# A list of 381 displacements in the issue order of a two-layer encoder

## The chip, the cores and the metric

The kernel runs on one core of a Trainium2 chip. The metric is the time of one execution on the device in microseconds, the median of several runs. One execution is profiled; its rows are what this document argues from. The engines are TensorE (PE; its weight loads are listed as PEld), VectorE (DVE), ScalarE (ACT), GpSimd (POOL) and SyncE (SP, which issues DMAs).

## The reference

Two transformer layers over 1024 tokens of width 1024, in float32. Layer 0 has two groups of heads: A, eight heads of grouped-query attention with normalised and rotated q and k, and B, eight heads of latent attention whose keys and values come from a 128-wide latent. Layer 1 has 16 heads of attention in a window of 128 tokens to each side, with a distance penalty and a sink. Both are gated by SiLU, and each layer has an adaptive normalisation in front.

```python
for layer in range(DEPTH):
    mod = c_act @ ada_w[layer] + ada_b[layer]
    shift, scale, gate = jnp.split(mod, 3, axis=-1)
    h = rms_norm(x, norm_w[layer]) * (1.0 + scale[:, None, :]) + shift[:, None, :]
    y = even_mixer(h, ...) if layer % 2 == 0 else odd_mixer(h, ...)
    x = x + gate[:, None, :] * y
return rms_norm(x, final_norm)
...
# one head of either group of layer 0
sc = jnp.einsum('bqkgd,bskd->bkgqs', qi, k).astype(jnp.float32) * scale
p = jax.nn.softmax(sc, axis=-1).astype(v.dtype)
o = jnp.einsum('bkgqs,bskd->bqkgd', p, v)
```

## The kernel before

**Numbers in two parts.** A float32 operand is split into a rounded part ("hi", fp32r) and the rest ("lo"). The name of a tile ends in h or l for them, or the two lie in one tile (hl, hla, hlb: 512 columns each). A product is then two or three fp32r matmuls.

**Stages.** Layer 0's input projections run first (to about 140 us), then the heads of group A (to about 425 us), those of group B (to about 650 us), the output projection of layer 0 in a scheme with seven instead of eight quarter products (`wino_out`), the projections and windowed heads of layer 1, and its output projection. `run_groups` treats half a head (512 queries) as a group. For each of its four blocks of 128 queries `softmax_unit` makes the scores S (matmuls into two PSUM banks), their negated row maximum nm (a reduction on DVE), the exponential P with its row sum sm (ACT), the reciprocal rs (DVE) and the scaling of P (POOL). For the group before, `pv_step` runs eight times: four transposes of P into a PSUM tile (named T), a cast to hi (ACT, left half of hla in group A and of hlb in group B), the rest lo (DVE, right half), and two matmuls with the values VA or VB into an accumulator pv. `pv_final` adds the accumulator's two halves (ot on ACT, og on DVE) and gates (POOL). Gate projections (gT), the modulation vectors (ada, adag: a reduction over a loaded tile on DVE), and group B's q and k halves (q, k, VB, qrt, cqTh) are filled in between.

**What sets the order.** No instruction is issued where the code writes it. A `Recorder` (`add`, `cost`, `run`) notes 9556 operations in the order of the code, each with its number i, its engine, an estimated duration and the operations that it depends on. `run` is a list scheduler: it plays the five engines with those durations, gives every engine the ready operation of lowest priority number, gives out PSUM banks and SBUF slots as they come free, and keeps an instruction of DVE with two SBUF inputs from starting while POOL is busy, and the reverse (`held`). What it returns is a start time for each operation. `emit` sorts by these starts, passes the sequence through `moved` and `banks_in`, and issues the operations in that sequence. Each engine runs its own operations strictly in that order, and an operation waits for its inputs and for the bank or slot that it writes.

**moved** (from line 488) takes the list `MOVES` of triples (kind, i, j). Kind 0 brings operation i forward to just before j, with all operations between them that i depends on; kind 1 puts i back to just after j, with all operations between them that depend on i:

```python
for kind, i, j in moves:
    lo, hi = (pos[j], pos[i]) if kind == 0 else (pos[i], pos[j])
    group, todo = {i}, [i]
    while todo:
        x = todo.pop()
        near = [d for d in self.ops[x].deps if d >= 0] if kind == 0 else [u for u, full in self.ops[x].users if full]
        for d in near:
            if d not in group and lo <= pos[d] <= hi:
                group.add(d)
                todo.append(d)
    here, rest = [x for x in part if x in group], [x for x in part if x not in group]
    seq[lo:hi + 1] = here + rest if kind == 0 else rest + here
```

**banks_in** walks the final sequence and keeps the bank that `run` gave to a PSUM tile where it is still free there, and else takes another free one (the one that has been free longest, for a pair of banks). So a displacement can also change the bank of a tile, and with it the instruction that the tile's first writer waits for.

In this kernel `MOVES` is empty: the sequence is the list scheduler's own, and every tile has the bank that `run` gave it. Since all operations are issued from one helper, all rows of the profile bear one line (L551); they are told apart by the names of their tiles.

Of the kernel before, what the change touches and what calls it, by code (L numbers as in the profile page):

```python
# [70 lines left out]
ADA_AT = (8, 5, ("c2", 6), 2, 4, 10, ("op", 1, 7), ("w", 2, 2))  # L71


MOVES = ()

SLOPES = [float(np.float32(2.0) ** np.float32(-8.0 * k / 16)) for k in range(1, 17)]

# [37 lines left out]
class Recorder:  # L115
# [427 lines left out]
    def emit(self):  # L543
        total = self.run()
        real = lambda v: v.real() if isinstance(v, VP) else v
        seq = self.moved([o.i for o in sorted(self.ops, key=lambda o: (o.start, o.i))], MOVES)
        self.banks_in(seq)
# [1506 lines left out]
```

## Time and profile before

| What | Value |
|---|---|
| Median of 3 runs | 1178.45 us (1177.72 to 1179.77) |
| The profiled execution's own time | 1180.8 us |
| Its span, first to last instruction | 1178.1 us |
| Mean granted clock of TensorE | 0.992 |
| Busy: PE, DVE, ACT, POOL | 1140.4, 948.4, 699.9, 599.9 us |
| DMA | 133.42 MB, mean 113 GB/s |

A row of the timeline or of a group reads: start (or count), duration, engine, line, operation, written tile<-read tiles, shapes, and in square brackets the idle time of the engine before it with what ended it. A row of windows reads: stretch, its length, then for PE, PEld, DVE, ACT and POOL the busy time with the number of instructions, then the granted clock of PE, the busy share of the DMA engines and the GB/s they moved. The waits that ended PE's idle time, summed by releaser over the heads of layer 0 (110 to 660 us), are:

```profile
PE psum L551 <- DVE hla L551: 6.5, 8, 1.7
PE psum L551 <- ACT Pa L551: 4.5, 5, 1.9
PE psum L551 <- DVE hlb L551: 1.5, 5, 0.5
PE psum L551 <- DVE q L551: 1.2, 3, 0.8
PE psum L551 <- ACT Pb L551: 1.0, 3, 0.4
```

The columns are the total in us, the number of waits and the longest one.

### The profile page before, as it was taken

Reading aid. Unit: us, or ns where it says so; the run is one execution under the profiler, and the core shown is the slowest. Engines: PE = TensorE matmul, PEld = TensorE weight load, DVE = VectorE, ACT = ScalarE, POOL = GpSimd, SP = SyncE. Lnnn points to the kernel's source line nnn. Section 1 sums busy time; section 2 is a strip of 40 time slices with the busy share of each in tenths; the row PEclk is TensorE's granted clock in tenths of the full one; section 3 lists DMA queues with packets and bytes.
Section 4 is the critical chain, followed back from the end, with each engine's and each line's share of the span. In section 5 each row is a group of like instructions: output and inputs, shape, how many; then the busy total and the mean of one; then the engine's idle time right before and its main releaser. Section 6 shows DMA issues by size and latency. Waiting matters only on the chain.

```text
span 1178.1 us, 17460 instructions
## 1 busy us (share of the span) xinstructions
PE 1140.4 (97%) x6070; PEld 957.6 (81%) x6070; DVE 948.4 (81%) x1678; ACT 699.9 (59%) x1406; POOL 599.9 (51%) x579
## 2 busy tenths in 40 slices
PE   7999999999999999999999999999999999999996
PEld 7898877878877878788877887988888888888885
DVE  8974889888887988888889988959776597765885
ACT  5553356565555777787778832327765365565723
POOL 1334496957854645554445444704465266445414
PEclk9999999999999999999999999999999999999998
DMA  9601433232221148786125333400002212036413
GB/s 368 253 1 66 163 117 125 90 111 89 84 63 54 52 116 222 186 217 175 37 88 225 117 143 125 161 19 8 31 18 91 72 37 90 19 144 237 139 35 143
DMA packets 41671, 133.42 MB, mean 113 GB/s; under 512 B 4592, under 2 KB 9200, under 8 KB 41584
## 3 DMA queue, kind: packets, MB, share of 16 engines
q1 hardware_dynamic: 38192, 122.88, 29.4%
q0 software_dynamic: 2304, 8.39, 4.2%
q8 instruction: 47, 0.77, 0.3%
q10 hardware_dynamic: 1088, 1.05, 0.3%
q14 instruction: 40, 0.33, 0.1%
HBM read 101.24 MB, written 31.06 MB: 112 GB/s over the span
## 4 chain that ended last, share of the span: by engine, by line
PE 77%; DVE 11%; ACT 5%; DMA 3%; issue 2%; POOL 1%; SPq 0%; POOLq 0%; ACTq 0%; DVEq 0%
PE psum L551 77%; DVE nm L551 2%; DMA ada<-in_ada_t 2%; DMA w2s<-in_w_c 1%; DMA w31s<-in_w_c 1%; ACT k L551 1%; DVE hla L551 1%; ACT Pa L551 1%; ACT q L551 1%; DVE adag L551 1%; DVE xr L551 1%; ACT Pb L551 1%; DVE hl L551 1%; DVE p L551 0%; DVE hlb L551 0%
## 5 line engine op out<-in xcount | busy, mean ns | idle before, releaser
L551 DVE TENSOR_REDUCE nm<-psum 128x1 f32<-128x1024 f32 x128 | 154.6, 1217 | 16.4 <-PE psum L551 14.7
L551 POOL TENSOR_SCALAR p<-p,dn 128x384 f32<-128x384 f32 (+1 forms) x128 | 71.8, 580 | 154.9 <-ACT p L551 74.6
L551 PE MATMUL psum<-hla,VA 128*128 128x512 f32 x256 | 94.1, 427 | 9.0 <-DVE hla L551 6.5
L551 POOL TENSOR_SCALAR Pa<-Pa,rs 128x1024 f32<-128x1024 f32 x64 | 78.9, 1238 | 43.4 <-DVE rs L551 41.3
L551 POOL TENSOR_SCALAR Pb<-Pb,rs 128x1024 f32<-128x1024 f32 x64 | 72.1, 1128 | 41.6 <-DVE rs L551 39.6
L551 ACT CAST hla<-psum 128x512 fp32r<-128x512 f32 x128 | 71.3, 596 | 36.8 <-PE psum L551 30.0
L551 PE MATMUL psum<-hlb,VB 128*128 128x512 f32 x256 | 90.9, 427 | 2.2 <-DVE hlb L551 1.5
L551 DVE TENSOR_TENSOR hla<-psum,hla 128x512 fp32r<-128x512 f32 x128 | 83.8, 681 | 11.3 <-ACT hla L551 10.9
L551 ACT ACTIVATE Pa<-psum,nm 128x1024 f32<-128x1024 f32 x64 | 71.6, 1121 | 33.6 <-DVE nm L551 28.4
L551 PE MATMUL psum<-ident,Pa 128*128 128x128 f32 x512 | 89.0, 273 | 1.0 <-DVE q L551 0.8
L551 ACT ACTIVATE Pb<-psum,nm 128x1024 f32<-128x1024 f32 x64 | 71.9, 1124 | 26.8 <-DVE nm L551 24.2
L551 DVE TENSOR_TENSOR hlb<-psum,hlb 128x512 fp32r<-128x512 f32 x128 | 81.9, 683 | 7.2 <-ACT hlb L551 5.8
L551 PE MATMUL psum<-k,q 128*128 128x512 f32 x256 | 84.3, 400 | 1.0 <-ACT Pb L551 1.0
L551 DVE CUSTOM_DVE_ANT_0 p<-psum,bias,rows_g 128x384 f32<-128x384 f32 (+1 forms) x128 | 70.2, 578 | 15.4 <-PE psum L551 12.4
L551 PE MATMUL psum<-ident,Pb 128*128 128x128 f32 x512 | 79.7, 272 | 1.0 <-DVE og('0', 7)_1184 L551 0.8
L551 ACT ACTIVATE p<-p,nm 128x384 f32<-128x384 f32 (+1 forms) x128 | 74.0, 584 | 4.0 <-DVE nm L551 3.9
L551 ACT CAST hlb<-psum 128x512 fp32r<-128x512 f32 x128 | 69.2, 603 | 9.1 <-PE psum L551 7.5
L551 ACT COPY ot<-psum 64x512 f32<-64x512 f32 x64 | 37.4, 584 | 61.5 <-PE psum L551 60.8
L551 PEld LDWEIGHTS psum<-ident,Pa 128*128 128x128 f32 x512 | 64.3, 141 | 11.8 <-DVE q L551 1.0
L551 PEld LDWEIGHTS psum<-ident,Pb 128*128 128x128 f32 x512 | 63.3, 140 | 12.8 <-DVE og('0', 7)_1184 L551 1.1
L551 ACT CAST hl<-psum 128x512 fp32r<-128x512 f32 x88 | 46.2, 592 | 31.3 <-PE psum L551 29.9
L551 PEld LDWEIGHTS psum<-hla,VA 128*128 128x128 f32 x256 | 46.7, 191 | 21.8 <-DVE hla L551 10.7
(890 smaller groups left out, 3639.0 us busy)
## 6 DMA issues: line engine op xcount, KB each, us to landing
ada<-in_ada_t SPq DMA_DIRECT2D x32, 512.0 KB, 6.9
adag<-in_ada_t SPq DMA_DIRECT2D x16, 512.0 KB, 5.1
ws<-in_w_out POOLq DMA_DIRECT2D x16, 512.0 KB, 5.7
ws<-ws SPq DMA_DIRECT2D x16, 512.0 KB, 3.3
S<-ws SPq DMA_DIRECT2D x16, 512.0 KB, 4.6
o<-spill SPq DMA_DIRECT2D x12, 512.0 KB, 5.3
A<-in_w_out SPq DMA_DIRECT2D x12, 512.0 KB, 5.8
xT<-in_xt SPq DMA_DIRECT2D x8, 512.0 KB, 8.1
```

What stands on the lines that cost most here:

```text
L551: fn(*[real(v) for v in a], **{k: real(v) for k, v in kw.items()})
```

## The change

The empty list gets 381 entries: 188 of kind 0 and 193 of kind 1. 262 of them move the named operation alone, the others take up to 12 more with it. 216 name an operation of PE, 106 one of DVE, 41 of ACT, 18 of POOL. They lie in all parts of the program; the most are in the heads of layer 0 and in the windowed heads of layer 1. No operation is added, removed or altered, and no other constant changes.

```diff
-MOVES = ()
+MOVES = (
+    (1, 1368, 1425), (1, 1601, 1652), (0, 2052, 1976), (1, 1362, 1375), (1, 2088, 2099), (1, 1663, 1755),
+    (1, 1930, 2012), (1, 1363, 1380), (1, 2221, 2225), (1, 2061, 2118), (1, 1435, 1319), (1, 1785, 1795),
...
+    (0, 3682, 3666), (1, 3147, 3133), (0, 3133, 3403), (1, 3445, 3438), (1, 4831, 4947), (1, 4833, 4948),
+    (1, 4940, 5013), (1, 1931, 1930), (0, 2564, 2408), (1, 3247, 3348), (1, 3288, 3133), (1, 3370, 3367),
+    (0, 3467, 3398), (1, 3437, 3501),
+)
```

In the numbering of the recorder, 1360 and 1368 are the first two casts of hla for the second group, 1425 the exponential Pa of the block that stands beside them, 1362 the first matmul with that hla, 1372 to 1375 four transposes; 2052 is the last transpose ahead of the cast 2053, 2061 a cast of hla and 2118 an exponential; 3247 the sum og at 402 us, 3340 the rest of hla at 406 us; 5762 the residual add in front of the squares at 721 us; 7953 the matmul that waits at 966 us.

59 rows, old and new, of the table MOVES are left out of this document.

## Prediction

> **What bounds the kernel now.** I read the page first, then the busy times by windows, then the waits and the timeline around every idle place of TensorE.
>
> ```profile
> span 1178.1 us, 17460 instructions
> PE 1140.4 (97%) x6070; PEld 957.6 (81%) x6070; DVE 948.4 (81%) x1678; ACT 699.9 (59%) x1406; POOL 599.9 (51%) x579
> ```
>
> PE is busy for 1140.4 of 1178.1 us. The change keeps all 17460 instructions and alters no shape, so it can only win what PE does not use: 37.7 us of idle time, and what a lowered clock costs. The windows say where that lies (length, then busy time of PE, PEld, DVE, ACT and POOL, then PE's granted clock):
>
> ```profile
> 0.00:20.00 20.00, 14.10 (x83) 12.88 (x84) 14.14 (x24) 10.07 (x16) 3.19 (x9) 0.91 0.90 350
> ...
> 141.00:270.00 129.00, 122.82 (x638) 99.42 (x636) 112.74 (x173) 78.82 (x142) 95.76 (x86) 0.97 0.33 112
> 270.00:400.00 130.00, 127.78 (x708) 105.34 (x706) 109.44 (x172) 80.53 (x152) 84.72 (x84) 1.00 0.22 71
> 400.00:432.00 32.00, 27.82 (x151) 21.51 (x150) 28.83 (x50) 24.38 (x47) 14.08 (x16) 1.00 0.38 115
> ...
> 480.00:540.00 60.00, 58.59 (x317) 47.36 (x316) 53.32 (x86) 47.83 (x89) 33.58 (x34) 1.00 0.80 203
> ...
> 595.00:607.00 12.00, 11.01 (x61) 7.86 (x60) 11.51 (x19) 9.96 (x19) 2.51 (x3) 1.00 0.43 171
> 607.00:650.00 43.00, 41.36 (x220) 33.60 (x219) 40.46 (x59) 35.16 (x60) 25.73 (x20) 1.00 0.44 165
> 650.00:722.00 72.00, 70.49 (x336) 58.53 (x335) 62.33 (x70) 36.61 (x50) 29.17 (x14) 1.00 0.33 121
> 722.00:960.00 238.00, 237.96 (x1291) 205.28 (x1290) 179.62 (x443) 130.61 (x325) 111.42 (x126) 1.00 0.19 65
> 960.00:990.00 30.00, 28.82 (x149) 23.76 (x148) 24.27 (x56) 16.56 (x45) 19.39 (x22) 1.00 0.20 71
> ...
> 1160.00:1178.20 18.20, 7.77 (x59) 6.57 (x57) 7.61 (x19) 5.12 (x12) 9.53 (x12) 0.76 0.34 115
> ```
>
> PE's idle time is the length less its busy time: 5.90 us at the head, 6.18, 2.22, 4.18, 1.41, 0.99, 1.64, 1.51, 0.04 and 1.18 in the windows between, 10.43 at the tail. Head and tail wait on a fixed chain (first loads, last normalisation, last store), so the field of play is about 19 us of idle time between 141 and 990, and one window whose clock was 0.97.
>
> **The change part by part.** Followed through the list's own rules, the 381 displacements leave SP's order as it was. Of 6070 PE instructions 325 stand out of their old order, of 1501 on DVE 86, of 1153 on ACT 37, of 573 on POOL 23; 68 of 872 PSUM tiles get another bank. Nothing is added or removed; every term below is a wait that gets longer or shorter.
>
> *First place, 171 us.* The rows are start, duration, engine, instruction, and in brackets the idle time before it.
>
> ```profile
> 167.26 3.48 DVE L551 TENSOR_REDUCE nm<-psum 128x1 f32<-128x1024 f32 x3
> 168.70 0.93 PE L551 MATMUL psum<-ident,Pa 128*128 128x128 f32 x7
> 169.23 1.07 ACT L551 CAST hla<-psum 128x512 fp32r<-128x512 f32 x2 [2.61 <-PE psum L551]
> 170.19 1.13 ACT L551 ACTIVATE Pa<-psum,nm 128x1024 f32<-128x1024 f32 x1
> 171.46 0.50 PE L551 MATMUL psum<-hla,VA 128*128 128x512 f32 x1 [1.83 <-ACT Pa L551]
> ...
> 172.00:176.50 4.50, 4.34 (x16) 3.27 (x15) 2.74 (x6) 2.08 (x5) 4.50 (x5) 0.62 0.00 0
> ```
>
> PE's seven transposes are over at 169.63; the next matmul starts at 171.46, once the exponential Pa has freed its bank. That exponential could start when the first of three reductions is done, 167.26 + 3.48/3 = 168.4, but ACT has it behind two casts of hla and sits idle for 2.61 us. The list puts the exponential ahead of both casts and four more transposes ahead of the matmul. Exponential from 168.5 to 169.7, cast to 170.3, matmul at about 170.35: 1.1 us earlier. PE's clock also fell after this wait: 0.62 over 4.5 us, so 0.38 x 4.5 = 1.7 us lost. With an idle stretch of well under a microsecond I expect no drop (650 to 722 holds a wait of 1.51 us, quoted below, at a clock of 1.00). Gain 2.8 (between 1.1 and 3.7).
>
> [...]
>
> *Second place, 257 us.*
>
> ```profile
> 254.95 0.58 ACT L551 COPY ot<-psum 64x512 f32<-64x512 f32 x1
> 255.56 1.11 ACT L551 ACTIVATE Pa<-psum,nm 128x1024 f32<-128x1024 f32 x1
> ...
> 256.82 0.50 PE L551 MATMUL psum<-khh,Qa 128*128 128x512 f32 x1 [1.95 <-ACT Pa L551]
> 257.16 0.40 PE L551 MATMUL psum<-kll,Qa 128*128 128x512 f32 x1
> 257.40 0.40 PE L551 MATMUL psum<-khh,Qa 128*128 128x512 f32 x1
> ...
> 258.00:262.00 4.00, 4.00 (x13) 3.11 (x12) 2.94 (x5) 1.89 (x4) 2.23 (x3) 0.57 0.00 0
> ```
>
> A matmul's record lasts 0.40 us while the next starts 0.24 later (257.16, 257.40), so a bracket shows a wait about 0.17 us short: here the wait is 2.1 us. The list takes the last transpose that feeds hla six places forward on PE (about 1.4 us of matmuls come between it and the waiting one) and one cast of about 0.5 us from ahead of the exponential: 1.9 of 2.1 us. The clock gives another 0.43 x 4.0 = 1.7. Against that, one matmul of the next block comes three places forward and needs a bank that the second exponential still reads; I take 0.9 us for it. Gain 2.7 (1.0 to 3.8). What else lies in the window 141 to 270 I put at 0.5.
>
> *400 to 432 us*, the deepest hole:
>
> ```profile
> 404.58 1.09 DVE L551 TENSOR_TENSOR qrt<-qrz,ropeb 128x128 f32<-128x128 f32 x1
> 406.33 0.50 PE L551 MATMUL psum<-hla,VA 128*128 128x512 f32 x1 [0.88 <-DVE hla L551]
> ...
> 417.69 0.69 DVE L551 TENSOR_TENSOR k<-psum,k 64x512 fp32r<-64x512 f32 x1 [0.61 <-ACT k L551]
> 418.41 1.23 DVE L551 TENSOR_REDUCE nm<-psum 128x1 f32<-128x1024 f32 x1
> 420.28 0.73 PE L551 MATMUL psum<-hla,VA 128*128 128x512 f32 x2 [1.34 <-DVE hla L551]
> ...
> 429.00 1.19 PE L551 MATMUL psum<-hla,VA 128*128 128x512 f32 x4 [0.78 <-DVE hla L551]
> ```
>
> PE waits for the rounding rest of hla, which stands on DVE behind work that nobody needs yet. The list puts this qrt (1.09) and an attention output (0.69) behind it: the 1.05 us at 406 go, and 0.3 before it. At 420, k and nm (0.69 + 1.23) step behind hla; of 1.5 us I count 0.9, since the exponential that follows nm then holds the next block. At 429 about 0.75 us of PE work is put in front. At 424 (0.78 us idle) a matmul comes forward that needs the bank of an exponential: nothing won. Gain 3.0 (1.5 to 4.5).
>
> *Two single places.*
>
> ```profile
> 710.99 0.74 DVE L551 SCALAR_TENSOR_TENSOR xr<-psum,gcol,xr 128x512 f32<-128x512 f32 x1
> 712.26 0.68 DVE L551 SCALAR_TENSOR_TENSOR b220l<-og('0', 7)_1184,b220h 128x512 fp32r<-128x512 f32 x1
> 720.93 0.63 PE L551 MATMUL psum<-ident,sq 128*128 128x128 f32 x4 [1.51 <-DVE sq L551]
> 966.49 0.72 PE L551 MATMUL psum<-hl,V 128*128 128x512 f32 x2 [1.09 <-DVE hl L551]
> ```
>
> At 721 the transposes wait for the squares of x1 (ACT, POOL, DVE in a row). The residual add at the head of that chain steps ahead of these two DVE instructions, 0.74 + 0.68 less their overlap: 1.2. At 966 the waiting matmul goes 28 places back, behind work that is ready: 1.3, all of it.
>
> *The smaller places* I take by share. 480 to 540: 1.0 of 1.41 (casts step behind exponentials). 595 to 607: 1.0, since the rests of hlb step ahead of five q and k halves, though one rest steps behind another. 270 to 400: 0.8; 607 to 650: 0.4. Part of these windows the list leaves alone:
>
> ```profile
> 197.97 0.50 PE L551 MATMUL psum<-hla,VA 128*128 128x512 f32 x1 [1.70 <-DVE hla L551]
> 368.65 1.06 POOL L551 TENSOR_SCALAR cqTh<-lat 128x1024 fp32r<-128x1024 f32 x1 [1.50 <-DMA lat<-lat_sp]
> 372.54 0.73 PE L551 MATMUL psum<-hla,VA 128*128 128x512 f32 x2 [1.05 <-DVE hla L551]
> 640.03 3.42 DVE L551 TENSOR_TENSOR b110l<-o,b110h 128x1024 fp32r<-128x1024 f32 x1
> ```
>
> At 198 DVE's order is the same, 1.70 us stay. At 372 cqTh steps ahead of a scaling of Pa on POOL, but it waited for a transfer, so 1.05 us stay. The 3.42 us rest at 640 keeps its place.
>
> Sum of the named terms: 2.8 + 2.7 + 0.5 + 3.0 + 1.2 + 1.3 + 1.0 + 1.0 + 0.8 + 0.4 = 14.7 us. Brackets hide up to 0.17 us a wait; some 20 of the smaller waits, at 0.12 each, add 2.4. New waits: checking each moved instruction's inputs against the slack it had, about a dozen places come out short by 0.1 to 0.8 us, 6 us in all if nothing gives, nothing if the engine before them has idle time to absorb it. I take 2.0, nearer to the lower end, since ACT and POOL are busy for only 59% and 51%. Net 14.7 + 2.4 - 2.0 = **15.1 us**. Against the profiled execution's 1180.8 us that is 1165.7; the timed median is 2.35 lower, 1178.45, so 1163.3.
>
> **The rivals.** *DVE gives it back (20%).* DVE is busy for 28.83 of 32.00 us in 400 to 432, 11.51 of 12.00 in 595 to 607, 40.46 of 43.00 in 607 to 650, and 112.74 of 129.00 in 141 to 270. Order does not shorten it: what steps back falls due some matmuls later. Then 3.0 + 1.0 + 0.4 and half of the first window's 6.0 return, 7.4 us: gain 7.7, 1170.7. For it: the high shares. Against it: what steps back (q, k, og) is used a whole head later.
>
> *Port collisions, slower (7%).* The 3.42 us of b110l stand against 1.21 us for a rest of the same shape when POOL is quiet:
>
> ```profile
> 709.86 1.21 DVE L551 SCALAR_TENSOR_TENSOR b220l<-o,b220h 128x1024 fp32r<-128x1024 f32 x1
> ```
>
> The planner keeps such DVE instructions apart from POOL's; the displacements undo its timing. Each new collision on PE's path costs 3.42 - 1.21 = 2.2 us, so seven eat the gain and eight make the kernel slower; ten give 1178.45 - 15.1 + 22 = 1185. Against it: only 23 POOL instructions move, and most rests read PSUM, not two SBUF tiles. [...]
>
> *It does nothing (7%).* If what ends each wait is a transfer or the latency of PE to ACT to DVE to PE, other order shows other brackets and the same end, 1178.4. For it: cqTh above. Against it: the rows at 171, 404 and 418 show queues, not latency.
>
> **How the numbers follow.** My forecast has 66%: 1163.3 us. Its own bounds: no new waits and the left-alone 372 and some small places gone too, 15.1 + 2.0 + 5 = 22, gives 1156; the lower ends of the two clock places (3.4 less) and 6 us of new waits give 1171. With the first rival's 1170.7 and a little more, the range is 1155.5 to 1172.5. A difference under 0.2% (2.4 us) can't be told from none by this measurement. Faster 86% (forecast and first rival), same 7%, slower 7%.
>
> **What would show it.** Right: no clock under 0.9 between 141 and 270; idle time in 400 to 432 under 2 us instead of 4.18; at 721 and 966 brackets under 0.5; the 198 bracket still near 1.7. Wrong: new brackets over 1 us at places that had none, or DVE rests of over 3 us where there were 1.2.

## The result, and the profile after

The changed kernel takes 1158.53 us (median of 4 runs, 1158.22 to 1158.68), the kernel before 1178.96 us beside it (4 runs, 1177.72 to 1179.77): a ratio of 0.9837 (0.9823 to 0.9852), 20.4 us faster. The forecast was 15.1 us, and its range held the time. The profiled execution took 1158.22 us, its span is 21.7 us shorter than that of before.

The page's line of the span and its busy times, changed kernel:

```profile
span 1156.4 us, 17461 instructions
PE 1129.6 (98%) x6070; PEld 956.1 (83%) x6070; DVE 939.4 (81%) x1678; ACT 700.5 (61%) x1406; POOL 596.4 (52%) x579
```

PE's idle time fell from 37.7 to 1156.4 - 1129.6 = 26.8 us. That is 10.9 of the 21.7 us. PE's busy time fell by 10.8, though it does the same work: a matmul at the lower clock has a longer record (0.63 us at 173.35 us in before, 0.40 for the same one in the changed kernel), and the part of a wait that its predecessor's record hides counts as busy (at 257.16 us of before a record lasts 0.40 us and the next one starts 0.24 us after its start). Two stretches of 3.41 us at half the clock (from 172.84 and 258.18 us) are gone, by an estimate 2 x 3.41 x 0.5 = 3.4 us of it. DVE's busy time fell by 9.0 us, also for the same instructions.

The windows of the changed kernel, on the stretches that hold the work of 141 to 270, 270 to 400, 400 to 432, 480 to 540, 595 to 607, 607 to 650, 650 to 722 and 960 to 990 us of before (start and end, length, busy time of PE, PEld, DVE, ACT and POOL, PE's clock):

```profile
143.00:265.00 122.00, 119.12 (x635) 96.85 (x636) 111.16 (x174) 78.20 (x143) 93.76 (x86) 1.00 0.35 117
265.00:391.60 126.60, 126.50 (x710) 105.83 (x708) 107.64 (x172) 81.09 (x152) 87.99 (x85) 1.00 0.22 72
391.60:419.10 27.50, 25.79 (x149) 21.12 (x148) 26.24 (x48) 24.04 (x46) 12.97 (x15) 1.00 0.44 134
468.00:528.00 60.00, 58.33 (x321) 48.10 (x322) 53.14 (x86) 47.77 (x90) 33.85 (x34) 1.00 0.78 202
582.00:592.00 10.00, 9.95 (x61) 7.84 (x60) 9.64 (x16) 8.89 (x17) 1.22 (x2) 1.00 0.50 202
592.00:633.00 41.00, 40.56 (x221) 33.38 (x220) 39.02 (x60) 35.25 (x61) 26.10 (x20) 1.00 0.45 173
631.00:703.00 72.00, 72.00 (x349) 60.05 (x348) 64.36 (x72) 38.79 (x54) 32.93 (x16) 1.00 0.34 121
940.60:969.00 28.40, 28.40 (x151) 24.03 (x150) 21.71 (x55) 16.19 (x43) 18.43 (x22) 1.00 0.16 58
```

PE's idle time is now 2.88, 0.10, 1.71, 1.67, 0.05, 0.44, 0.00 and 0.00 us, where it was 6.18, 2.22, 4.18, 1.41, 0.99, 1.64, 1.51 and 1.18. Every one of these stretches filled up but one, 480 to 540. The first begins behind a new wait at 142.86 us, so the 2.88 leave it out. The clock of the first is 1.00 where it was 0.97.

For a finer account I matched the same matmul in both traces at some two dozen points and took the difference of the distances between them, which counts idle time, hidden waits and clock alike:

| Stretch (us of before) | Forecast gain | Measured |
|---|---|---|
| start to 141, with the new wait at 142.86 | 0 | -1.9 |
| 141 to 190 (the place at 171) | 2.8 | 3.4 |
| 190 to 265 (the place at 257, and "the rest") | 3.2 | 3.5 |
| 265 to 385 | 0.8 | 3.4 |
| 385 to 432 | 3.0 | 4.6 |
| 432 to 540 | 1.0 | 0.0 |
| 540 to 607 | 1.0 | 2.5 |
| 607 to 650 | 0.4 | 1.9 |
| 650 to 722 | 1.2 | 1.6 |
| 722 to 960 | 0 | 0.7 |
| 960 to the end | 1.3 | 2.2 |
| hidden in brackets, less new waits | 0.4 | (in the rows) |

The column sums to 21.8 us. The waits that ended PE's idle time over the heads of layer 0 in the changed kernel (total, number, longest):

```profile
PE psum L616 <- DVE gT L616: 2.3, 2, 1.7
PE psum L616 <- DVE hlb L616: 2.0, 4, 1.1
PE psum L616 <- DVE hla L616: 1.9, 2, 1.7
PE psum L616 <- ACT hla L616: 1.0, 1, 1.0
PE psum L616 <- ACT Pa L616: 0.5, 1, 0.5
PE psum L616 <- ACT Pb L616: 0.4, 1, 0.4
```

The rests of hla fell from 6.5 to 1.9 us, and of the 1.9 one wait is 1.7: the place at 198, which the prediction left standing. The exponentials Pa fell from 4.5 to 0.5. On top of the list stands a name that had 0.3 before, gT: a new wait. The timeline of the changed kernel shows it, and the two first places:

```profile
142.86 0.50 PE L616 MATMUL psum<-khh,Qa 128*128 128x512 f32 x1 [1.68 <-DVE gT L616]
...
169.01 1.11 ACT L616 ACTIVATE Pa<-psum,nm 128x1024 f32<-128x1024 f32 x1
170.81 0.59 ACT L616 CAST hla<-psum 128x512 fp32r<-128x512 f32 x1 [0.60 <-PE psum L616]
171.43 1.09 PE L616 MATMUL psum<-ident,Pa 128*128 128x128 f32 x8 [0.66 <-DVE gT L616]
172.28 0.48 PE L616 MATMUL psum<-hla,VA 128*128 128x512 f32 x1
196.41 0.50 PE L616 MATMUL psum<-hla,VA 128*128 128x512 f32 x1 [1.70 <-DVE hla L616]
251.98 0.66 PE L616 MATMUL psum<-ident,Pa 128*128 128x128 f32 x4 [0.28 <-DVE Qa L616]
252.70 0.50 PE L616 MATMUL psum<-khh,Qa 128*128 128x512 f32 x1
```

At 171 the exponential now stands ahead of the cast, as forecast, and the matmul with hla (172.28) has no bracket: what is left is 0.66 us in front of the transposes. At 252.70 the matmul that waited 1.95 us starts without a wait.

### The profile page after: what moved, and what is told of

Read it like the earlier page. It is cut to its first block, busy times and chain, and to the rows that moved or that the text cites. A ratio compares the mean times of both kernels' runs of the same rounds, so it can differ in the third digit from the quotient of the medians.

```text
span 1156.4 us, 17461 instructions
## 1 busy us (share of the span) xinstructions
PE 1129.6 (98%) x6070; PEld 956.1 (83%) x6070; DVE 939.4 (81%) x1678; ACT 700.5 (61%) x1406; POOL 596.4 (52%) x579
## 4 chain that ended last, share of the span: by engine, by line
PE 87%; DVE 5%; DMA 4%; ACT 1%; issue 1%; POOL 1%; SPq 0%; POOLq 0%; DVEq 0%; ACTq 0%
PE psum L616 87%; DVE nm L616 2%; DMA ada<-in_ada_t 2%; DMA w2s<-in_w_c 1%; DMA w31s<-in_w_c 1%; DVE hlb L616 1%; DVE Qa L616 1%; DVE ada L616 0%; DVE hla L616 0%; DMA q<-qr_sp 0%; POOL Pb L616 0%; SPq L616 0%; DVE q L616 0%; ACT Pb L616 0%; POOL xr L616 0%
## 5 line engine op out<-in xcount | busy, mean ns | idle before, releaser
L616 POOL TENSOR_SCALAR Pa<-Pa,rs 128x1024 f32<-128x1024 f32 x64 | 81.4, 1278 | 39.3 <-DVE rs L616 31.7
L616 PE MATMUL psum<-hla,VA 128*128 128x512 f32 x256 | 91.0, 419 | 3.0 <-DVE hla L616 1.9
L616 PE MATMUL psum<-hlb,VB 128*128 128x512 f32 x256 | 88.4, 424 | 0.5 <-DVE hlb L616 0.5
L616 DVE TENSOR_TENSOR hl<-psum,hl 128x512 fp32r<-128x512 f32 x88 | 56.1, 684 | 10.0 <-ACT hl L616 9.5
```

The source lines that it names most:

```text
L616: fn(*[real(v) for v in a], **{k: real(v) for k, v in kw.items()})
```

## The experiments

My theory was that the gain is local: each displacement takes away, or makes, a wait at its own place, and the places add up. Rivals were that an earlier end of one stretch shifts the later ones into or out of collisions (then parts don't add up), that one engine's order alone carries the gain, and that collisions of DVE and POOL decide. Six kernels keep some of the entries, two make one displacement alone, two improve the list, one repeats it. None leaves work out.

### The list in four parts

The parts go by the operation that the entry names (the second number of the triple): before 2140 (68 entries), 2140 to 3509 (95), 3510 to 5239 (128), from 5240 (90).

```diff
-MOVES = (... 381 entries)
+MOVES = tuple(m for m in ALL if LOW <= m[1] < HIGH)
```

> Only the 68 entries that name an operation below 2140 (up to about 260 us). Local theory (each place gains by its own displacements, nothing else): what the two traces show up to there, -5.0 us (171 us: 3.0; 257 us: 3.1; a new wait at 142 us costs 2.0). Phase theory (what a place loses hangs on which of DVE and POOL starts first there, and any shift upstream changes that): places behind 270 us change as well, and the total can be anything from -2 to -9; b110l at 640 us, which no entry here touches, would no longer take 3.42 us.

> Only the 95 entries that name an operation from 2140 to 3509 (about 270 to 430 us). Local theory: -7.9 us, of it 4.3 in 400 to 432 us and 1.25 at 372 us. Phase theory: places behind 430 us change too, and the four parts don't add up to 20.4 us.

> Only the 128 entries that name an operation from 3510 to 5239 (about 430 to 630 us). Local theory: -2.3 us, of it 2.1 in 595 to 607 us; b110l at 640 us stays at 3.42 us. Phase theory: b110l gets its 1.2 us here or in one of the earlier parts.

> Only the 90 entries that name an operation from 5240 on (630 us to the end). Local theory: -6.5 us, of it 2.0 at 640 us, 1.7 at 721 us, 1.5 in 960 to 990 us; no entry moves b110l or the POOL work beside it, so if the 2.0 us at 640 us are won here they come from the PE order. Phase theory: 640 us keeps its 3.42 us and its waits of 0.83 and 0.38 us, -4.5 us; the sum of the four parts is off from 20.4 us by over 3 us.

Against 1178.37 us on that chip they took 1172.99, 1172.63, 1176.12 and 1172.48: ratios 0.9950 (0.9938 to 0.9961), 0.9948 (0.9936 to 0.9960), 0.9974 (0.9964 to 0.9984), 0.9954 (0.9937 to 0.9971). The gains, 5.4 + 5.7 + 2.3 + 5.9 = 19.3 us, add up to within 1.1 us of the whole list's 20.4. By its interval each of them is known to between 1.2 and 2.0 us, so the sum cannot be told from the whole. The parts need little of each other, as the local theory has it; whether each gain also arises at its own place is another question, which the traces answer below. Part 2 gave 5.7 us where 7.9 was expected, the others came within 0.6 us of the local theory's figure. By matched matmuls the first part holds the places at 171 and 257 (3.4 and 3.5 us) and also the wait at 143 (-2.0); the second 3.1 of the 4.6 us at 385 to 432 (its trace has the clock at 0.95 there, the changed kernel 1.00); the third 2.1 us at 595 to 607; the fourth 1.7 at 721 and 1.2 at 966.

The trace of part 4 is 8.4 us ahead of before at the end, and 4.5 us of that were won at four places where this part has no entry: 1.5 at 171, 0.9 at 265 to 290, 0.7 at 360 to 385 and 1.4 at 628 to 650. So not all of the gain is local. At 171 the wait is the old one. The timeline and some windows of part 4, then of part 3, which has no entry there either:

```profile
171.51 0.50 PE L567 MATMUL psum<-hla,VA 128*128 128x512 f32 x1 [1.83 <-ACT Pa L567]
...
166.91:170.32 3.41, 2.76 (x16) 2.14 (x14) 3.41 (x4) 1.05 (x3) 3.41 (x5) 1.00 0.37 154
170.32:173.73 3.41, 2.06 (x10) 1.57 (x11) 2.02 (x6) 3.41 (x8) 3.41 (x5) 1.00 0.00 0
173.73:177.15 3.42, 3.42 (x26) 2.96 (x25) 2.76 (x5) 2.31 (x5) 3.00 (x3) 1.00 0.00 0
```

```profile
171.32 0.51 PE L574 MATMUL psum<-hla,VA 128*128 128x512 f32 x1 [1.83 <-ACT Pa L574]
...
169.28:172.69 3.41, 1.43 (x8) 0.90 (x7) 2.37 (x6) 3.41 (x7) 3.41 (x4) 1.00 0.01 4
172.69:176.11 3.42, 3.42 (x10) 2.55 (x10) 1.99 (x4) 1.24 (x3) 3.42 (x4) 0.50 0.00 0
```

The same bracket, 1.83 us, stands before a clock of 1.00 in the one and of 0.50 in the other. The windows are cut where these traces change the clock: each change comes a whole number of 3.41 us after the others of its trace (in before the drops begin at 15.83, 172.84 and 258.18 us, 46 and 25 times 3.413 apart). In part 3 the whole wait falls into one such window, and PE is busy for 1.43 us of it; in part 4 an edge cuts the wait, and PE is busy for 2.76 and 2.06 us. It goes this way in all seven traces with this bracket: at most 1.43 us busy in the four that drop, at least 1.9 in each window in the three that do not. So in these seven traces the drop at this place goes with where the wait falls in the windows, which differed between parts 3 and 4 though neither has an entry there; no entry was needed to win it.

The stretch 265 to 290 goes with a modulation vector (adag) at 268 us. It takes 3.12 to 3.32 us beside POOL in the five traces that won nothing there (before, parts 2 and 3, both single displacements) and 1.27 to 1.55 in the eight that won 0.8 to 1.0. The other two stretches, 360 to 385 and 628 to 650, are taken up with the single displacements below.

### One engine's entries at a time

```diff
-MOVES = (... 381 entries)
+MOVES = tuple(m for m in ALL if engine(m[1]) == "PE")   # pe_alone
+MOVES = tuple(m for m in ALL if engine(m[1]) != "PE")   # others_alone
```

Entries that find no place without the others are left out: 210 of 216 and 163 of 165 remain. The split is not quite clean, as an entry takes along what hangs on it: PE's entries displace 288 instructions of PE, 6 of DVE and 3 of ACT, the others 82 of DVE, 36 of ACT, 23 of POOL and 47 of PE.

> Only entries that name a PE operation (210 of 216; six no longer apply without the others). By the prediction's terms, places won by PE work put in front (257, 429, 966 us and the four transposes at 171 us) keep about 5 us; places won by another order on ACT, DVE and POOL (404, 420, 595, 721 us, the exponential at 171 us) stay. Rival: the two kinds need each other, and each alone brings less than half of its share.

> Only entries that name an operation of ACT, DVE or POOL (163 of 165). By the prediction's terms about -9 us: 404, 420, 595 and 721 us lose their brackets, and the exponential at 171 us ends 1.1 us earlier. Rival: less than -5 us, since the PE order holds the waiting matmul where it was.

Measured, against 1178.38 us: PE's entries alone 1186.1, ratio 1.0067 (1.0055 to 1.0080), 7.7 us *slower*; the others alone 1172.59, ratio 0.9952 (0.9938 to 0.9966), 5.8 us faster. I had expected 5 us of gain from the first; that was wrong in sign. From the second I had expected 9 us. Alone they make +1.9 us, together -20.4, so some 22 us come from having both. By matched matmuls PE's entries alone lose 4.5 us at 480 to 540 and 3.2 behind 990, and the others lose 2.5 and 2.4 at 480 to 540 and 960 to 990. The waits of PE over the heads of layer 0 say how. PE's entries alone:

```profile
PE psum L587 <- DVE hla L587: 6.0, 7, 1.7
PE psum L587 <- ACT Pa L587: 4.7, 5, 2.1
PE psum L587 <- DVE hlb L587: 3.6, 7, 1.0
PE psum L587 <- ACT Pb L587: 3.5, 5, 2.4
```

All the others alone:

```profile
PE psum L580 <- DVE hla L580: 3.3, 4, 1.7
PE psum L580 <- DVE gT L580: 2.6, 3, 1.7
PE psum L580 <- ACT Pb L580: 2.4, 3, 1.6
```

With PE's order alone nothing that PE waited for comes earlier (hla 6.0, Pa 4.7, as before), and matmuls that were brought forward now ask for banks that an exponential still reads: Pb goes from 1.0 us to 3.5. With the other engines' order alone hla falls to 3.3 and Pa to 0.7, but Pb stands at 2.4, probably since what was put behind on ACT or DVE is now asked for too early. Only both together bring hla to 1.9 and Pb to 0.4. The timelines show one such wait each, first of PE's entries alone, then of the others alone:

```profile
500.16 0.73 PE L587 MATMUL psum<-k,q 128*128 128x512 f32 x2 [2.38 <-ACT Pb L587]
```

```profile
967.18 0.66 PE L580 MATMUL psum<-ident,p 128*128 128x128 f32 x4 [1.47 <-POOL p L580]
```

### Single displacements: the places that the prediction left alone

At 640 us the rest b110l took 3.42 us beside a POOL instruction. The whole list moves neither, yet the stretch gained 1.9 us. The theory of collisions says that the POOL instruction won by starting first; then one entry that puts it (5463) behind 5264 on the kernel before must win the place by itself. At 372 the list puts a scaling of Pa on POOL (2969) behind 2985, so that cqTh steps ahead of it, and the prediction said that this gains nothing, as cqTh waits for a transfer; the wait went all the same.

```diff
-MOVES = ()
+MOVES = ((1, 5463, 5264),)   # t101_late
+MOVES = ((1, 2969, 2985),)   # cqTh_first
```

> The kernel before with one displacement: POOL's subtraction t101 goes behind the next gating product, out of the way of b110l on DVE; nothing that PE waits for depends on t101 before 700 us. Collision theory (b110l waits out t101 because both read SBUF and t101 began first): b110l takes 1.2 instead of 3.42 us, the brackets of 0.83 and 0.38 us at 645 us go, -1.2 to -2.0 us. Order theory (the gain at 640 us comes from what was displaced there): no change.

> The kernel before with one entry of the list, the scaling Pa611 put behind two later ones, so that cqTh stands ahead of it on POOL (4 of 573 positions change, no other engine). The prediction: cqTh waits for its transfer anyway, no change. Collision theory: the scaling that follows cqTh on POOL begins after cqTl on DVE and not before it, cqTl takes 1.2 instead of 2.14 us, the bracket of 1.05 us at 372 us goes: -1.0 to -1.3 us.

Each changes the order on POOL alone and the bank of no tile. The first took 1176.83, ratio 0.9987 (0.9978 to 0.9996), 1.55 us faster. The second 1179.08, ratio 1.0008 (0.9999 to 1.0018), no difference. The timeline of the first:

```profile
639.19 1.22 DVE L553 TENSOR_TENSOR b110l<-o,b110h 128x1024 fp32r<-128x1024 f32 x1
```

b110l takes 1.22 us and not 3.42, as the POOL instruction now begins at 643.80. In before it began at 639.93, 0.10 us ahead of b110l at 640.03:

```profile
639.93 2.44 POOL L551 TENSOR_TENSOR t<-o,o 128x1024 f32<-128x1024 f32 x1
```

In the changed kernel DVE came to the place earlier, ahead of a scaling that precedes this POOL instruction:

```profile
623.48 3.31 POOL L616 TENSOR_SCALAR Pb<-Pb,rs 128x1024 f32<-128x1024 f32 x2
624.55 1.25 DVE L616 TENSOR_TENSOR b110l<-o,b110h 128x1024 fp32r<-128x1024 f32 x1
...
626.76 2.38 POOL L616 TENSOR_TENSOR t<-o,o 128x1024 f32<-128x1024 f32 x1
```

Of the two POOL scalings the second began 30 ns behind b110l and took 2.21 us instead of 1.15, while b110l lost nothing. Against POOL's work b110l stands some 1.2 us earlier than in before, where it began 1.19 us after this scaling. So the 3.42 us hung on which engine came first, and the list tipped that by the way. In the trace of part 4 b110l takes 2.01 us, which goes with the 1.4 us won there.

At 372 the entry is not the cause. That stretch (360 to 385) gained 1.25 us with the whole list, 0.5 to 1.15 in parts 1, 3 and 4, none of which has an entry near it, 0.45 in part 2, which holds this one, and 0.6 to 0.7 in the two single displacements. PE waits there for a rest of hla that stands on DVE behind the rest cqTl, in before and in the changed kernel:

```profile
369.75 2.14 DVE L551 TENSOR_TENSOR cqTl<-lat,cqTh 128x1024 fp32r<-128x1024 f32 x1 [0.60 <-POOL cqTh L551]
362.26 1.23 DVE L616 TENSOR_TENSOR cqTl<-lat,cqTh 128x1024 fp32r<-128x1024 f32 x1 [0.25 <-POOL cqTh L616]
```

What each trace won there is, to 0.05 us, what cqTl ended earlier against the matmuls around it. Behind cqTh, cqTl and a scaling of Pa on POOL start within 70 ns of each other in all 13 traces, POOL's record first. In five the scaling takes 1.12 to 1.13 us and cqTl 2.13 to 2.14; in eight the scaling takes 2.19 and cqTl 1.23. The changed kernel and its repeat are among the eight, the last kernel below (without_13_ada_late) among the five. So 0.9 us at this place are an outcome of the execution and not of the list; the rest is when the transfer in front of cqTh lands.

### A better list

The wait at 143 (2.0 us between matched matmuls) came with part 1 and with the entries of the engines other than PE. On DVE a residue of the gate projection (gT) now stands behind a modulation vector (ada), Qa and nm:

```profile
138.84 1.28 DVE L616 CUSTOM_DVE_ANT_0 ada<-ada,cb,cols 128x1024 f32<-128x1024 f32 x1
...
140.14 0.69 DVE L616 SCALAR_TENSOR_TENSOR Qa<-psum,Qa 64x512 fp32r<-64x512 f32 x1
140.87 1.23 DVE L616 TENSOR_REDUCE nm<-psum 128x1 f32<-128x1024 f32 x1
142.12 0.69 DVE L616 SCALAR_TENSOR_TENSOR gT<-gT,psum 128x512 f32<-128x512 f32 x1
```

PE needs the bank that this gT reads. One kernel drops the 13 entries that name operations 990 to 1145; another puts in addition the modulation vector that DVE has ahead of the rest at 198 behind operation 1529. The list itself was run once more beside them.

```diff
 MOVES = (... 381 entries
-    (0, 1022, 1052), (0, 1126, 1132), (1, 1061, 1124), (1, 1119, 1061), ... 13 of them
+    (1, 1612, 1529),   # without_13_ada_late only
 )
```

> The changed kernel once more, beside the next two on the same chip: both theories expect 1158 to 1159 us.

> The list without the 13 entries that name an operation from 990 to 1145, among which must be what makes the new wait of 1.68 us at 143 us (a matmul waits for gT, which stands behind four longer DVE instructions). Local theory: -2.0 us against the list, 1156.5 us. Rival (the DVE work that those entries brought forward falls due later): the same as the list, 1158.5 us.

> The same and one more entry: the modulation reduction ada141 goes behind the second rest of hla on DVE, so that the matmul that stays 1.7 us idle at 198 us in the kernel before (196 us in the changed one) no longer waits for it. Local theory: another -1.9 us, 1154.6 us. Rival: ada141 meets the scalings of POOL at its new place and blocks the next rests, another 0 us.

Against 1179.01 us: the list 1158.23, ratio 0.9829 (0.9815 to 0.9843); without the 13 entries 1157.17, 0.9819 (0.9805 to 0.9833); with the later ada 1155.80, 0.9808 (0.9795 to 0.9822). The first step gains 1.1 us over the list and the second 1.4 more, 2.4 together; 2.0 and 1.9 had been expected. The intervals against the kernel before overlap, but the runs themselves do not: 1157.88 to 1158.68 for the list, 1155.62 to 1156.44 for the last kernel. By matched matmuls the place at 143 gave back its whole 2.0 us. The profiled execution of that kernel was also 1.9 us behind before at 30 us, of which 1.3 came back by 100; this head differs by up to 1.9 us between executions. At 198 the 1.70 us are gone, and two rests further on a wait of 0.93 us has come:

```profile
196.50 0.73 PE L614 MATMUL psum<-hla,VA 128*128 128x512 f32 x2 [0.93 <-DVE hla L614]
```

So the list left at least two places unsolved, and the last kernel is the fastest of those run.

## Why the prediction was right, point by point

- **PE's idle time and clock are the field of play: right.** PE keeps 26.8 us idle, mostly head and tail. Half of the gain shows as idle time, the other half as shorter records.
- **171 and 257 (2.8 and 2.7): right, a little low.** Measured 3.4 and 3.5. The lower clock at 257 (0.50 from 258.18 to 261.59 us in before) came in all seven traces that keep that wait. At 257 I had taken off 0.9 us for a bank that an exponential holds; what came is a bracket of 0.28. But the 1.7 us of clock in the first is not a firm part of the gain: of seven traces with a bracket of 1.83 us at this place, four (before, part 3, both single displacements) have the lower clock behind it, three (parts 2 and 4, PE's entries alone) have not. The mixed outcome goes with the windows of 3.41 us: 1.83 us of idle time within one came four times with the lower clock behind it, cut by an edge it came three times without.
- **400 to 432 (3.0): right in kind, low.** 4.6 of a bound of 4.5. Idle time fell to 1.71 us, under the 2 that I had named, and the rest lies in hidden waits.
- **721 and 966 (1.2 and 1.3): right.** 1.7 and 1.5 at the places themselves. Both matmuls start without a bracket.
- **595 to 607 (1.0): low.** 2.1 at the place, more than the 0.99 us of idle time that I took it from: hidden waits again.
- **270 to 400 (0.8): much too low.** 3.4 us, more than the 2.22 us that stood there as idle time. This is the step that failed most: I took the small places "by share" of the brackets, and the lengths of DVE's instructions as given. Of the 3.4 us, 0.9 came at 268, where adag became shorter, and 1.25 at 372, where cqTl did. The other 1.25, at 290 to 360, is more than the brackets there show: each hides up to 0.17 us, and I had added 2.4 us for that in one lump.
- **480 to 540 (1.0): wrong.** Nothing came of it. Against what the casts won stands a new wait at the start of that stretch, 1.24 us from start to start:

```profile
468.71 0.33 PE L616 MATMUL psum<-ident,Pb 128*128 128x128 f32 x1 [1.09 <-DVE hlb L616]
```

- **"Left alone": right at 198, wrong at 640, and at 372 right about the entry but not about the place.** At 640 I read a long rest as a fixed cost that goes only if one of the two is moved. It was the outcome of which engine came first.
- **New waits (2.0): low, and in other places.** 2.0 at 143 and 1.24 at 468, where a dozen short ones had been counted. So a sign that I had named for being wrong, new brackets over 1 us, came twice (1.68 and 1.09 us) though the forecast held; the other, long rests of DVE where there were short ones, did not, and all four signs for being right did.
- **Collisions, the slower rival: wrong in sign.** That rests which read PSUM keep out of collisions, one of my two reasons against, the trace of before shows: its 256 rests of hla and hlb took 0.66 to 0.69 us each, while POOL was busy for 51% of the span. DVE's busy time fell by 9.0 us and POOL's by 3.5. The modulation vector adag at 268 us shows a part of it, before and after:

```profile
267.99 3.14 DVE L551 CUSTOM_DVE_ANT_0 adag<-adag,cb,g 128x1024 f32<-128x1024 f32 x1
262.96 1.53 DVE L616 CUSTOM_DVE_ANT_0 adag<-adag,cb,g 128x1024 f32<-128x1024 f32 x1
```

- **DVE gives it back: no.** It is busy for 26.24 of 27.50 us in the hardest stretch, a larger share than before, and PE waits less there.

By matched matmuls the sum was 21.8 - 15.1 = 6.7 us short. The small places (265 to 385 and 540 to 650) gave 7.7 us where I had 2.2, 5.5 too little; the other stretches behind 141 us were 3.4 too low together; the start and the 0.4 of the last row took 2.3 back. The main mechanism was right: waits go place by place. The mis-sized terms are those that were read off brackets by share, and a second mechanism had a price as a loss alone: at 268, 372 and 640 a DVE instruction beside POOL became shorter (3.14 to 1.53, 2.14 to 1.23 and 3.42 to 1.25 us), and these three places gave 4.0 of the 21.8 us. The 0.9 of them at 372, and 1.5 us of clock at 171, are luck of the profiled executions. No run separates the order from the 68 tiles that change their bank, so what the banks add is open.

## What to carry to other kernels

Here one engine was busy for 97% of the span, and the order of issue was still worth 1.7% (1178.96 to 1158.53 us), found place by place: gains and losses of separate places add up, within 1 to 2 us here. Meetings of DVE with POOL are the exception here: at 372 starts within 70 ns of each other gave 2.13 to 2.14 us for DVE's instruction in five traces and 1.23 in eight. Move the waiting instruction and the work it waits for together; the same moves on one engine alone cost 7.7 us or gave 5.8, and both gave 20.4. And measure a wait from start to start of the same instructions in two traces, since brackets hide a part of each (up to 0.17 us by the rows at 257).

## What the hardware showed that I had not expected

- The lower clock after a wait of 1.83 us at 171 goes with windows of 3.41 us that run on through the whole execution (in before the clock falls at 15.83, 172.84, 258.18 and 1169.54 us, 46, 25 and 267 times 3.413 apart): four times the wait fell into one window, PE was busy for at most 1.43 us of it, and the next 3.41 us had half the clock; three times an edge cut it, PE was busy for at least 1.9 us of each, and the clock stayed at 1.00. Where the border lies is open: at 413 us in part 2 half the clock followed a window with 1.87 us busy.
- In the two meetings of b110l with POOL that are shown above, the later one paid: b110l took 3.42 us when it was 0.10 us behind and 1.25 when it was 0.03 ahead, with the POOL scaling at 2.21 instead of 1.15. The close case is at 372: POOL's record is first by 48 to 69 ns in all 13 traces, and DVE paid in five (2.13 to 2.14 us instead of 1.23), POOL in eight (2.19 instead of 1.12 to 1.13).
